# Loads issued from ScalarE's queue at written places, squares summed by DMA where rows are made, and a hand-written end, in a one-layer hybrid attention trunk

## The chip, the core and the metric

The kernel runs on one core of a Trainium2 chip. The core has TensorE (matrix products, fp32 in PSUM), VectorE, ScalarE, GpSimd and SyncE, called PE, DVE, ACT, POOL and SP in the profile, and 16 DMA engines. SP, ACT and POOL can issue transfers. The metric is the device time of one execution in microseconds (us); less is better.

## The reference, cut to what matters

The program is one layer of a decoder for 1024 positions and width 2048, in fp32:

```python
hn = rmsnorm(h, norm_mix_g)
sb_q, sb_k, sb_v, sb_g, df_q, df_k, df_v, df_g = split(hn @ w_in)
sb_out = stick_breaking_attention(sb_q, sb_k, sb_v)          # 8 heads of 128
df_out = rmsnorm(differential_attention(rope(df_q), rope(df_k), df_v, lam), subln_g)
mixed = concat([sb_out * silu(sb_g), df_out * silu(df_g)])
h = h + mixed @ w_out
gate = sigmoid(rmsnorm(h, norm_ple_g) @ w_ple_gate)
h = h + gate * (p @ w_ple_proj)
return rmsnorm(h, norm_final_g)
```

All the change touches, but for one line, lies behind the attention: the product with `w_out`, the gate with its norm, and the final norm. A norm needs the mean of the squares over all 2048 columns of a row of `h`.

## The kernel before, in words

Everything is kept transposed: a tile has 128 columns of the model on its partitions and 512 positions (a half) on its free axis. `h` is 16 such tiles ("rows" below) for each of two halves, in a DRAM tensor `h_d`. So a sum of squares over the width is a sum over 16 tiles and then over the partitions; the latter is a product with a matrix of ones (`norm`, `mean`).

**Products.** fp32 operands are split into a high part (a cast on ScalarE) and a low part (a subtraction on VectorE), and each product is three TensorE instructions: high by high, low by high, high by low. The large products (value and gate columns, `w_out`, `w_ple_gate`) use a scheme with seven block products in place of eight, named A11, A12, S2, S1, S3, A22 and S4; S1 to S4 are made of sums of operands or differences of weights (`T1` to `T4`). One block product of a unit is 4 by 3 = 12 instructions of 128x512.

**Stages.** (1) The value and gate columns (`gv`, to about 340 us). (2) Input projection and attention, to about 1790 us. (3) `w_out` (`op`, two passes `ph` of eight units `u`): pass 0 adds the first half of the width, pass 1 the second. In pass 1 each unit makes four finished rows of `h`, put to `h_d` by GpSimd's queue (`put`). `sums` makes the combinations S1 to S4 of these rows for the gate and stores them in `hcomb_d`. (4) The gate. Half 1's products A11 and A12 (`p1`, `p2`, `gate1`), then S2, S1, S4 (`p6`, `p5`, `p3`), then half 0's S3 and A22 (`begin` and the loop over six units). (5) The end: units 6 and 7 in quarters of 256 positions (`partly`), the final norm (`rstd_from`) and the outputs (`final`, `final1`).

**Order.** The class `Seven` holds the order. `prod` (or `gprod` in the gate) writes a product and then calls `step`: one more weight block is cast (`whigh`, ScalarE) and one block's low part made (`wlow`, VectorE), about six blocks ahead of use; then the entries of `soon` that are due run (`due`), and two or three entries of `xq`, the queue of operands to be split, each with the slot from which it may run. TensorE's order is as written all through (a `manual_schedule`), VectorE's and ScalarE's in stages 1, 3 and 4, too. SP's and GpSimd's order is made by a planner from modelled times and priorities, and in the end (from line 1955) so is VectorE's and ScalarE's. An engine runs its instructions in order, transfers it issues included: one that waits holds up all behind it.

**Places that the change and the steps touch.** Before the change:

- Line 1024 (`gv`) and line 1582 (`op`): in pass 0, the results `b` and `c` of a unit are two PSUM tiles of the pool `acc` if `u % 3 == 2`, otherwise the two halves of one tile `bc` (pool `z`). In unit 0 product S1 (into `c`) follows S2 (into `b`) directly; the sum `u2` (lines 1031, 1590) reads `b` after S2, and S3 goes on in `b`.
- `load_operand` (1281) issues an operand's load from SP. Lines 1621 to 1623 load the eight operands A11 and A12 of pass 1 in units 1 to 4.
- `gate_operand` and `gate_loads` (1303 to 1335) load the gate's operands from SP. For A11 and A12 their split also squares the row on ScalarE (1320, 1325) and adds it to `ssh[1]` on VectorE (the line 747 of the profile, from which `soon` is run). `NEXT` lists which loads follow which last product of pass 1.
- Lines 1627 to 1630 load four gate weight blocks (`second_load`) and the operands A12 4 to 7 and S1 0 to 3 behind the last product of pass 1.
- `squares0` (1729) loads a row of half 0 from `h_d` again, squares it on ScalarE, and `add_squares` (1669) adds it to `sq_d` by an accumulating transfer from GpSimd's queue.
- The end from line 1957: both quarters in a loop, with the eight outputs of the first quarter written by `final` between the second quarter's last products and its root.

Of the kernel before, what the change touches and what calls it, by code (L numbers as in the profile page):

```python
# [13 lines left out]
F32 = mybir.dt.float32  # L14
# [6 lines left out]
P = 128  # L21
# [31 lines left out]
def _body(ctx, nc, tc, ap):  # L53
# [491 lines left out]
    with tc.tile_pool(name="at", bufs=2) as at, tc.tile_pool(name="pz", bufs=2, space=PSUM) as pz:  # L545
# [461 lines left out]
        for ph in range(2):  # L1007
            for u in range(H):
# [269 lines left out]
        sq_d = dram.tile([2, 2, P, HALF], F32, name="sq_d", tag="sq_d")  # L1278
        SUMS = "S1", "S2", "S3", "S4"

        def load_operand(ph, nm, i):
# [6 lines left out]
            nc.sync.dma_start(lo.bitcast(F32), src)  # L1288
# [10 lines left out]
        NEXT = {"A11": [("A11", 0)], "A12": [("A12", 0)], "S1": [("A11", 4)], "S3": [("S2", 0)]}  # L1299
# [4 lines left out]
        def gate_operand(nm, i):  # L1304

            hi, lo = op.places(GPLACE[nm][i], "g" + nm)
            raw = lo.bitcast(F32)
# [6 lines left out]
            nc.sync.dma_start(raw, src)  # L1314

            def fn():
                if nm in ("A11", "A12"):
                    if 1 not in ssh:
                        ssh[1] = ev.tile([P, HALF], F32, name="ssh", tag="rstd1", bufs=1)
                        A.activation(ssh[1], raw, AF.Square)  # L1320
                    else:
                        for j in range(2):
                            o = slice(j * 2 * P, j * 2 * P + 2 * P)
                            s = ev.tile([P, 2 * P], F32, name="s", tag="sm", bufs=5)
                            A.activation(s, raw[:, o], AF.Square)
# [3 lines left out]
            return fn  # L1329

        def gate_loads(nm, i0):
            e = [(op.slot + 2, gate_operand(nm, i0 + j)) for j in range(4)]
# [4 lines left out]

        def put(o, ph, hf, ch):

            if ph:  # L1340
                G.dma_start(h_d[hf, ch], o)
            else:
# [223 lines left out]
        for ph in range(2):  # L1566
            for u in range(8):
# [14 lines left out]
                if ph == 0 and u % 3 == 2:  # L1582
# [83 lines left out]

        nsq = [0, 0]

        def add_squares(half, s):

            n = nsq[half]
            nsq[half] += 1
            G.dma_start(sq_d[half, n % 2], s, **(dict(accum_op=ALU.add) if n > 1 else {}))
# [55 lines left out]
        def squares0(n):  # L1729

            for ch in (n,):
                t = ev.tile([P, HALF], F32, name="hs", tag=("rstd0", "ssq")[n % 2], bufs=1)
                nc.sync.dma_start(t, h_d[0, ch])

                def fn(t=t):
                    A.activation(t, t, AF.Square)
                    add_squares(0, t)

                op.soon.append((op.slot + 3, fn))

# [4 lines left out]
        embedding_load(1, "f")  # L1745
        p1(2)
        gate_loads("S2", 4)
        p2(1)
        norm([ssh[1]])
# [7 lines left out]
        squares0(0)  # L1757
        p2(2)
        gate1(0)
        squares0(1)  # L1760
        p1(4)
        gate1(1)
        squares0(2)
        p2(3)
        gate1(2)
        squares0(3)
        p1(5)
        gate1(3)
        squares0(4)
        p2(4)  # L1770
        gate1(4)
        squares0(5)
        p1(6)
        squares0(6)
        p2(5)
        gate1(5)
        squares0(7)
        p1(7)
        second_places()
        squares0(8)  # L1780
        p2(6)
        gate1(6)
        squares0(9)
        p2(7)
        gate1(7)
        squares0(10)
# [34 lines left out]
        for u in range(8):  # L1821
# [3 lines left out]
            if 11 + u < 16:  # L1825
                squares0(11 + u)
# [42 lines left out]
        def final(ts, r):  # L1869
# [197 lines left out]
```

## Time and profile before

| what | value |
|---|---|
| median of 3 runs | 2481.51 us (2480.61 to 2482.8) |
| the profiled execution's own time | 2478.19 us |
| its span, first to last instruction | 2476.4 us |
| granted TensorE clock over the span | 0.988 |
| moved by DMA | 459.89 MB, mean 186 GB/s |

The span is the time from the first to the last instruction of the profiled execution; the rest of its own time lies around it. A line of the profile names a line of the kernel, an engine, an operation, what it writes and reads, and how often and how long. The granted clock is the share of TensorE's full clock that a throttle allowed; it falls to a half for a while after TensorE was idle.

### The profile page before, as it was taken

What the parts mean: (1) busy time and instruction counts of PE and PEld (TensorE: products, weight loads), DVE (VectorE), ACT (ScalarE), POOL (GpSimd) and SP (SyncE); (2) the same over time, 40 slices, a digit from 0 to 9 for tenths busy, and PEclk for the clock granted to TensorE, in tenths of its full rate; (3) what the DMA queues carried; (4) which work ended last, traced back from release to release, by engine and by line L of the source; (5) the groups of instructions that cost most, each with busy time, mean ns of one, the idle gap of its engine ahead of it and who ended that gap; (6) DMA issues with size and microseconds to landing.
All of it is one profiled execution on the core that took longest, in us unless ns stands there. A gap on an engine that the chain in (4) does not pass through costs nothing.

```text
span 2476.4 us, 32496 instructions
## 1 busy us (share of the span) xinstructions
PE 2374.1 (96%) x11250; PEld 1967.5 (79%) x11250; DVE 1905.4 (77%) x3288; ACT 1199.1 (48%) x2151; POOL 231.0 (9%) x353
## 2 busy tenths in 40 slices
PE   8999999999999999999999999998889998989997
PEld 5777878888888887888888888886768886868886
DVE  6788767777877778788888878778567888567787
ACT  5343335555556445555655555445423325532454
POOL 1211110000000000000000001110111110111100
PEclk9999999999999999999999999999989999999998
DMA  8776754443455556343443344555768768899964
GB/s 292 251 257 227 227 174 151 152 157 124 140 149 147 181 162 200 98 129 114 119 120 115 102 122 125 145 135 179 208 158 199 230 221 313 246 328 326 333 201 168
DMA packets 213828, 459.89 MB, mean 186 GB/s; under 512 B 23904, under 2 KB 36448, under 8 KB 213664
## 3 DMA queue, kind: packets, MB, share of 16 engines
q1 hardware_dynamic: 163696, 336.95, 41.6%
q0 software_dynamic: 41904, 106.19, 16.9%
q10 hardware_dynamic: 8064, 14.68, 1.6%
q8 instruction: 88, 1.44, 0.2%
q14 instruction: 76, 0.62, 0.1%
HBM read 323.51 MB, written 142.61 MB: 188 GB/s over the span
## 4 chain that ended last, share of the span: by engine, by line
PE 78%; DMA 8%; DVE 7%; ACT 3%; issue 3%; SPq 0%; POOL 0%; ACTq 0%; DVEq 0%; POOLq 0%
PE acc L227 13%; PE acc L229 13%; PE acc L228 13%; PE pbc L614 4%; PE pbc L616 4%; PE pbc L615 4%; PE tp L402 2%; PE z L306 1%; PE z L305 1%; PE pa L615 1%; PE pa L616 1%; PE pa L614 1%; PE av L449 1%; PE av L448 1%; PE pb L1639 1%
## 5 line engine op out<-in xcount | busy, mean ns | idle before, releaser
L227 PE MATMUL acc<-xh,whi 128*128 128x512 f32 x1152 | 465.2, 404 | 2.5 <-ACT xh L1104 2.5
L229 PE MATMUL acc<-xh,wlo 128*128 128x512 f32 x1152 | 451.3, 392 | 2.2 <-DVE wlo L154 2.2
L228 PE MATMUL acc<-xl,whi 128*128 128x512 f32 x1152 | 450.6, 391 | 0.3 <-DVE xl L1105 0.3
L154 DVE TENSOR_TENSOR wlo<-wraw,whi 128x1024 fp32r<-128x1024 f32 x192 | 234.2, 1220 | 48.5 <-ACT whi L153 47.1
L153 ACT CAST whi<-wraw 128x1024 fp32r<-128x1024 f32 x192 | 201.7, 1051 | 120.7 <-PE acc L228 112.0
L710 ACT CAST wpr<-T 128x512 fp32r<-128x512 f32 x144 | 87.3, 621 | 354.5 <-DVE T L669 289.5
L229 PEld LDWEIGHTS acc<-xh,wlo 128*128 128x128 f32 x1152 | 216.4, 188 | 51.1 <-DVE wlo L154 3.5
L227 PEld LDWEIGHTS acc<-xh,whi 128*128 128x128 f32 x1152 | 217.0, 188 | 40.6 <-ACT xh L1104 2.9
L228 PEld LDWEIGHTS acc<-xl,whi 128*128 128x128 f32 x1152 | 217.4, 189 | 37.9 <-DVE xl L1105 0.6
L421 ACT CAST awh<-tp 128x256 fp32r<-128x256 f32 (+1 forms) x160 | 80.7, 504 | 153.9 <-PE tp L402 153.9
L357 ACT ACTIVATE et<-z,mx 128x512 f32<-128x512 f32 (+7 forms) x128 | 94.7, 740 | 61.2 <-DVE mx L351 52.7
L710 ACT CAST wpr<-wraw 128x512 fp32r<-128x512 f32 x112 | 68.6, 614 | 105.6 <-DMA wraw<-tw_d 36.3
L426 DVE TENSOR_TENSOR awl<-tp,awh 128x256 fp32r<-128x256 f32 (+1 forms) x160 | 92.4, 578 | 32.2 <-ACT awh L421 31.9
L724 DVE TENSOR_TENSOR wpr<-T,wpr 128x512 fp32r<-128x512 f32 x144 | 98.7, 686 | 7.4 <-ACT wpr L710 6.1
L614 PE MATMUL pbc<-cS,wpr 128*128 128x512 f32 x224 | 88.4, 395 | 14.3 <-DVE u L1590 12.6
L351 DVE TENSOR_REDUCE mx<-z 128x1 f32<-128x512 f32 (+7 forms) x128 | 97.0, 758 | 4.4
L336 DVE TENSOR_TENSOR_SCAN st<-pt 128x511 f32<-128x511 f32 (+3 forms) x64 | 86.7, 1354 | 17.6 <-ACT pt L329 16.0
L724 DVE TENSOR_TENSOR wpr<-wraw,wpr 128x512 fp32r<-128x512 f32 x112 | 75.6, 685 | 21.9 <-ACT wpr L710 21.8
L615 PE MATMUL pbc<-cS,wpr 128*128 128x512 f32 x224 | 88.1, 393 | 0.0
L616 PE MATMUL pbc<-cS,wpr 128*128 128x512 f32 x224 | 88.1, 393 | 0.0
L449 PE MATMUL av<-awl,v 128*128 128x256 f32 x256 | 73.7, 288 | 9.0 <-DVE awl L426 9.0
L329 ACT ACTIVATE pt<-z 128x512 f32<-128x512 f32 (+3 forms) x64 | 41.6, 650 | 77.6 <-DVE z L313 72.1
(535 smaller groups left out, 6170.2 us busy)
## 6 DMA issues: line engine op xcount, KB each, us to landing
wraw<-w_in SPq DMA_DIRECT2D x192, 512.0 KB, 3.6
wraw<-w_gate SPq DMA_DIRECT2D x96, 256.0 KB, 6.0
wraw<-w_out SPq DMA_DIRECT2D x72, 256.0 KB, 4.0
wraw<-w_vg SPq DMA_DIRECT2D x71, 256.0 KB, 4.2
comb_d<-sg POOLq DMA_DIRECT2D x48, 256.0 KB, 7.2
h_d<-hc POOLq DMA_DIRECT2D x48, 256.0 KB, 4.5
spare<-xT SPq DMA_DIRECT2D x44, 256.0 KB, 3.9
hc<-h_d SPq DMA_DIRECT2D x33, 256.0 KB, 5.3
```

The lines of the kernel that those rows point to most:

```text
L153: side.later(1, lambda: A.copy(hi[:, o], raw[:, o]))
L154: side.later(side.wlo, lambda: V.tensor_tensor(lo[:, o], raw[:, o], hi[:, o].bitcast(F32), op=ALU.subtract))
L227: T.matmul(acc[c], hi[:, k2, kh, c, :], xh, start=first, stop=False)
L228: T.matmul(acc[c], hi[:, k2, kh, c, :], xl, start=False, stop=False)
L229: T.matmul(acc[c], lo[:, k2, kh, c, :], xh, start=False, stop=last)
L351: V.reduce_max(mx, z[:, vw], axis=AX.X, negate=True)
L449: T.matmul(av, vv[:, 0, blk % 4, :], wl, start=False, stop=last)
L614: T.matmul(o, wh[:, w], xh, start=start and k == 0, stop=False, skip_group_check=True)
L615: T.matmul(o, wh[:, w], xl, start=False, stop=False, skip_group_check=True)
L616: T.matmul(o, wl[:, w], xh, start=False, stop=k == 3, skip_group_check=True)
L710: A.copy(t[:, 0], src)
L724: V.tensor_tensor(t[:, 1], src, t[:, 0].bitcast(F32), op=ALU.subtract)
```

## The change

It has five parts.

1. In `gv` and `op`, pass 0 gives two separate PSUM tiles to units 0, 3 and 6 and not to 2 and 5.
2. Twenty-four loads are issued from ScalarE's queue, at the places where they stand in its written order: the eight operands of pass 1 (in units 1 to 4 of pass 0), the gate's operands S2 0 to 3, S2 4 to 7 and S1 0 to 3, and four gate weight blocks. The operands and the weight blocks stood before at the end of pass 1 (S2 4 to 7 after `p1(2)`), on SP's queue, and now stand after `p1(2)`, `plew(0, 0)`, `gate1(1)` and `gate1(3)`.
3. The squares of every row are made in pass 1, one slot after its `put` (`row_squares`), from the tile that is being stored, and added up in `sq_d` by accumulating transfers: half 1's in a new third place, half 0's in place 0. The squares and adds in `gate_operand` and all of `squares0` go. Half 1's sums are loaded as two tiles (`load_sums(2, ...)`) ahead of `norm`.
4. A11 and A12 of the gate are split three slots after their load, not two.
5. The end is in the manual order for VectorE and ScalarE, too: the four half-tiles of each quarter go step by step (`begun`, `sigm`, `ended`, `squared`), ScalarE's tables are loaded by name, four of half 1's outputs (`late`) and the first quarter's outputs are put between the steps, and unit 7's projection weights are loaded earlier.

```diff
-                if ph == 0 and u % 3 == 2:
+                if ph == 0 and u % 3 == 0:
-        sq_d = dram.tile([2, 2, P, HALF], F32, name="sq_d", tag="sq_d")
+        sq_d = dram.tile([3, 2, P, HALF], F32, name="sq_d", tag="sq_d")
-        def load_operand(ph, nm, i):
+        def load_operand(ph, nm, i, eng=nc.sync):
...
-            nc.sync.dma_start(lo.bitcast(F32), src)
+            eng.dma_start(lo.bitcast(F32), src)
...
-        NEXT = {"A11": [("A11", 0)], "A12": [("A12", 0)], "S1": [("A11", 4)], "S3": [("S2", 0)]}
+        NEXT = {"A11": [("A11", 0)], "A12": [("A12", 0)], "S1": [("A11", 4)]}
...
-            def fn():
-                if nm in ("A11", "A12"):
-                    if 1 not in ssh:
-                        ssh[1] = ev.tile([P, HALF], F32, name="ssh", tag="rstd1", bufs=1)
-                        A.activation(ssh[1], raw, AF.Square)
-                    else:
-                        for j in range(2):
-                            o = slice(j * 2 * P, j * 2 * P + 2 * P)
-                            s = ev.tile([P, 2 * P], F32, name="s", tag="sm", bufs=5)
-                            A.activation(s, raw[:, o], AF.Square)
-                            op.soon.append((op.slot + 1, partial(V.tensor_tensor, ssh[1][:, o], ssh[1][:, o], s, op=ALU.add)))
-                op.split("g" + nm, i, hi, lo, gain, apart=True)
+            eng.dma_start(lo.bitcast(F32), src)
+            return partial(op.split, "g" + nm, i, hi, lo, gain, apart=True)
-        def gate_loads(nm, i0):
-            e = [(op.slot + 2, gate_operand(nm, i0 + j)) for j in range(4)]
+        def gate_loads(nm, i0, eng=nc.sync):
+            e = [(op.slot + (3 if nm in ("A11", "A12") else 2), gate_operand(nm, i0 + j, eng)) for j in range(4)]
...
+        def add_squares(k, s):
+            n = nsq[k]
+            nsq[k] += 1
+            G.dma_start(sq_d[k, n % 2], s, **(dict(accum_op=ALU.add) if n > 1 else {}))
+
+        def row_squares(hf, o):
+            n = nsq[3]
+            nsq[3] += 1
+            t = ev.tile([P, HALF], F32, name="rsq", tag=f"rstd{n % 2}", bufs=1)
+            A.activation(t, o, AF.Square)
+            add_squares(2 * hf, t)
...
             if ph:
                 G.dma_start(h_d[hf, ch], o)
+                op.soon.append((op.slot + 1, partial(row_squares, hf, o)))
...
-                        xq.append((op.slot + 3, load_operand(1, nm, i)))
+                        xq.append((op.slot + 3, load_operand(1, nm, i, A)))
...
-            second_load(0, 0, b)
         gate_loads("A12", 4)
-        gate_loads("S1", 0)
...
+        sums2 = load_sums(2, ((ev, "rstd1", 1), (ev, "ssq", 1)))
         p1(2)
-        gate_loads("S2", 4)
+        gate_loads("S2", 0, A)
         p2(1)
-        norm([ssh[1]])
+        norm(sums2)
+        ssh[1] = sums2[0]
...
-        squares0(0)
+        gate_loads("S2", 4, A)
         p2(2)
         gate1(0)
         p1(4)
         gate1(1)
+        gate_loads("S1", 0, A)
         p2(3)
         gate1(2)
         p1(5)
         gate1(3)
+        for b in (12, 11, 22, 21):
+            A.dma_start(raws[0, 0, b], wg(0, 0, b))
...
+        partly(6, "A22", 1)
+        finals(0, (0,))
+        ended(6, 1, 1)
+        ended(7, 1, 1)
+        squared(6, 1, 1)
+        squared(7, 1, 1)
+        begun(6, 0, 1)
+        sigm(6, 0, 1)
+        partly(7, "A22", 1)
+        mean(1, (6, 1), (7, 1))
+        finals(0, (1, 2))
+        ended(6, 0, 1)
+        squared(6, 0, 1)
+        begun(7, 0, 1)
+        sigm(7, 0, 1)
+        tables(LOGS)
+        finals(0, (3,))
+        ended(7, 0, 1)
+        squared(7, 0, 1)
+        mean(1, (6, 0), (7, 0))
+        finals(0, (4, 5, 6, 7))
+        root(1)
+        finals(1, range(8))
```

In the end, `begun` adds the product to its other part and multiplies by the root of the gate's norm (two VectorE operations), `sigm` is the sigmoid (ScalarE), `ended` multiplies by the projected embedding and adds the row (two VectorE operations), and `squared` squares it (ScalarE, the last one VectorE).

More of the change, by code (lines that the diff above doesn't have):

```diff
@@ L1888, in fn @@
                 nc.sync.dma_start(ap["out"][ch * P:ch * P + P, HALF:], t)
-            op.soon.append((op.slot + 3, fn))
+            if u_ < 5:
+                op.soon.append((op.slot + 3, fn))
+            else:
+                late.append(fn)
+        late = deque()
         def gating0(u, c, o, z):
@@ L2013, in _body, with begun, sigm, ended @@
-        final(ts, r2)
+        def begun(u, c, tq):
+            ts = TQ[tq]
+            o = qs[u][c][:, ts]
+            V.tensor_tensor(o, b[u], o, op=ALU.add)
+            V.tensor_tensor(o, o, ssh[0][:, ts], op=ALU.mult)
+        def sigm(u, c, tq):
+            o = qs[u][c][:, TQ[tq]]
+            A.activation(o, o, AF.Sigmoid)
+        def ended(u, c, tq):
+            ts = TQ[tq]
+            o, t = qs[u][c][:, ts], hpair[u][:, c, ts]
+            V.tensor_tensor(o, o, z[u][:, c, ts], op=ALU.mult)
+            V.tensor_tensor(t, t, o, op=ALU.add)
@@ new lines, in squared, with mean @@
+        def squared(u, c, tq):
+            t = hpair[u][:, c, TQ[tq]]
+            s = sqs[u, c, tq] = ev.tile([P, Q], F32, name="sq", tag="sm", bufs=5)
+            if (u, c, tq) == (7, 0, 1):
+                V.tensor_tensor(s, t, t, op=ALU.mult)
+            else:
+                A.activation(s, t, AF.Square)
+        def mean(tq, *es):
+            first = tq not in ms
+            if first:
+                ms[tq] = pp.tile([P, Q], F32, name="ssps", tag="t")
+                T.matmul(ms[tq], ones, s2[:, TQ[tq]], start=True, stop=False)
+            for e in es:
+                T.matmul(ms[tq], ones, sqs.pop(e + (tq,)), start=False, stop=e == (7, 0))
@@ new lines, in tables, with root, finals @@
+        def tables(nm):
+            A.preload_act_table_set(nm)
+        r = ev.tile([P, HALF], F32, name="r2", tag="rstd1", bufs=1)
+        rt = ev.tile([P, HALF], F32, name="r3", tag="sq", bufs=2)
+        def root(tq):
+            rstd_from(ms[tq], 1.0 / NK, eps6, EPS, r[:, TQ[tq]], rt[:, TQ[tq]])
+        def finals(tq, us):
+            for u in us:
+                final(TQ[tq], r[:, TQ[tq]], u)
+        LOGS, SIGS = "natural_log_exp_and_others", "sigmoid_and_others"
+        partly(6, "S3", 0)
@@ new lines, in _body @@
+        for c in (1, 0):
+            ple(0, 6, c, z[6][:, c, :])
+        begun(6, 1, 0)
+        sigm(6, 1, 0)
+        partly(7, "S3", 0)
+        for c in (1, 0):
+            ple(0, 7, c, z[7][:, c, :])
+        begun(7, 1, 0)
+        ended(6, 1, 0)
+        late.popleft()()
+        squared(6, 1, 0)
+        sigm(7, 1, 0)
+        partly(6, "A22", 0)
+        ended(7, 1, 0)
+        late.popleft()()
+        begun(6, 0, 0)
+        squared(7, 1, 0)
+        sigm(6, 0, 0)
+        partly(7, "A22", 0)
@@ new lines, in _body @@
+        ended(6, 0, 0)
+        late.popleft()()
+        begun(7, 0, 0)
+        squared(6, 0, 0)
+        sigm(7, 0, 0)
+        tables(LOGS)
+        partly(6, "S3", 1)
+        ended(7, 0, 0)
+        squared(7, 0, 0)
+        late.popleft()()
+        begun(6, 1, 1)
+        partly(7, "S3", 1)
+        mean(0, (6, 1), (7, 1), (6, 0), (7, 0))
+        root(0)
+        tables(SIGS)
+        begun(7, 1, 1)
+        sigm(6, 1, 1)
+        sigm(7, 1, 1)
+        partly(6, "A22", 1)
+        finals(0, (0,))
```

123 lines of the change are left out of this document (31 added, 92 removed).

## The prediction, made before the result was known

> **What bounds the kernel now.** I read the page first, then the table of stretches (to see where TensorE falls short of its steady count), then TensorE's waits, and last the timelines around each wait.
>
> ```profile
> span 2476.4 us, 32496 instructions
> PE 2374.1 (96%) x11250; PEld 1967.5 (79%) x11250; DVE 1905.4 (77%) x3288; ACT 1199.1 (48%) x2151; POOL 231.0 (9%) x353
> ```
>
> TensorE is busy 96% of the span, and the diff removes none of its large products. So only the remaining holes can be won. Profile time is 2478.19 us (span 2476.4 and 1.8 around it). The median of the three runs is 2481.51, 3.3 us above; I make the sum against 2478.2 and add 3.3 at the end.
>
> ```profile
> 1780.00:1800.00 20.00, 12.97 (x59) 10.34 (x57) 6.67 (x11) 5.31 (x10) 4.30 (x5) 0.95 1.04 286
> 1800.00:1820.00 20.00, 13.71 (x50) 11.15 (x51) 12.94 (x21) 5.67 (x11) 0.84 (x1) 0.71 0.30 79
> ```
> ```profile
> 2060.00:2080.00 20.00, 15.53 (x60) 12.09 (x59) 15.98 (x31) 11.05 (x26) 2.32 (x5) 0.91 1.04 391
> 2080.00:2100.00 20.00, 15.22 (x57) 11.32 (x57) 17.23 (x33) 15.54 (x32) 0.00 (x1) 0.87 0.76 249
> ```
> ```profile
> 2120.00:2140.00 20.00, 20.00 (x90) 16.57 (x89) 12.94 (x23) 11.95 (x22) 3.08 (x5) 1.00 0.72 233
> ```
> ```profile
> 2180.00:2200.00 20.00, 16.00 (x64) 12.65 (x63) 10.53 (x18) 8.14 (x16) 3.07 (x4) 0.91 1.07 358
> 2200.00:2220.00 20.00, 14.77 (x56) 11.12 (x55) 18.34 (x31) 9.16 (x17) 4.59 (x7) 0.91 1.03 306
> ```
>
> Each row is a stretch of 20 us: busy time and count of PE, PEld, DVE, ACT and POOL, then granted clock, DMA share, GB/s. A full stretch holds 90 products (2120 to 2140), 0.222 us each. The stretch from 2060 holds 30 fewer (6.7 us lost), from 2080 33 fewer (7.3), from 2180 26 (5.8), from 2200 34 (7.6). In four of the six short stretches the DMA share is 1.03 or more: the holes sit where transfers queue.
>
> ```profile
> PE pbc L614 <- DVE u L1590: 12.6, 1, 12.6
> PE ssps L2004 <- ACT sq L2001: 5.5, 2, 4.4
> PE pa L1640 <- DVE cgA12l L601: 4.8, 3, 3.8
> PE pbc L614 <- DVE hq L1616: 4.7, 2, 3.7
> PE pb L1641 <- DVE wpr L724: 4.2, 2, 3.5
> PE z L1562 <- ACT pwhl L1554: 4.0, 1, 4.0
> ```
>
> These six names are nearly all of TensorE's waits after 1790 us. I call them hole A (u L1590), C (hq L1616), D (cgA12l), E (pwhl), F (wpr), and the tail (sq L2001).
>
> **The change, part by part.**
>
> *Two banks apart for unit 0 (`u % 3 == 0`).* In unit 0 the products S2 and S1 follow each other directly, and today their two results are halves of one tile. First the value-gate phase:
>
> ```profile
> 67.36 0.47 PE L614 MATMUL pbc<-cS,wpr 128*128 128x512 f32 x1 [1.33 <-ACT cS4h L593]
> ```
>
> This first product of S1 starts just after L1031 has read the other half; its own weights and operands were there before. The profile names an ACT cast that ended at the same moment, so I read the tile as the cause from the code. Apart, S1 goes at once and S3 behind it finds the read done: 1.3 us (between 0, if the cast was the cause, and 1.3).
>
> *Hole A: the same edit, and the eight loads that leave SP.*
>
> ```profile
> 1806.29 0.77 PE L614 MATMUL pbc<-cS,wpr 128*128 128x512 f32 x1 [12.64 <-DVE u L1590]
> ```
> ```profile
> 1811.54 0.39 PE L614 MATMUL pbc<-cS,wpr 128*128 128x512 f32 x1
> ```
>
> ```profile
> 1801.11 0.69 DVE L669 TENSOR_TENSOR T<-wraw 128x512 f32<-128x512 f32 x1 [8.51 <-issue]
> ```
> ```profile
> 1805.46 0.68 DVE L1590 TENSOR_TENSOR u<-pbc,s 128x512 f32<-128x512 f32 x1
> ```
>
> S1 waits for the sum L1590 in VectorE's order, and L1590 stands 5.0 us (1801.11 to 1806.14) behind a weight difference that waits for a `w_out` block. That block's transfer, among the issues of 1783 to 1792:
>
> ```profile
> cA11l<-mixed_d SPq DMA_DIRECT2D x4, 256.0 KB, 5.2
> cA12l<-mixed_d SPq DMA_DIRECT2D x4, 256.0 KB, 9.9
> ```
> ```profile
> wraw<-w_out SPq DMA_DIRECT2D x1, 256.0 KB, 10.6
> ```
>
> The block took 10.6 us behind eight operands of the second pass, which the planner had put ahead of it. After the change these eight are issued from units 1 to 4. What one load costs the 16 DMA engines comes from 2100 to 2200 us:
>
> ```profile
> q1 hardware_dynamic: 12421, 19.33, 57.9%
> q0 software_dynamic: 1904, 3.93, 19.7%
> ```
>
> 57.9 us for 19.33 MB is 0.785 us per 256 KB, so eight are 6.3 us. The difference starts at about 1795, L1590 ends at 1800.3, and S3, which truly needs that read, starts at 1800.5. Today S3 starts at 1811.54, after S1's twelve products at half speed. That is 11.0 us. S1 ends at 1796.3 (S2 ended at 1793.65, twelve products of 0.222 follow), and the 4.2 us left idle will still slow the clock: I take 1.8 us, which is what the clock of 0.91 costs in the 20 us from 2060, behind a hole of 3.7. That leaves 9.2. Bounds: 2.6 if the block lands as late as now (S1's 5.25 us fall into the hole, and S3's products are slow instead), 11.0 if none is slow.
>
> *Squares made where rows are made.* Holes C and D are where VectorE and ScalarE add up squares on arrival, today (2045 to 2100 us):
>
> ```profile
> L747 DVE TENSOR_TENSOR ssh<-ssh,s 128x256 f32<-128x256 f32 x30 | 11.3, 420 | 2.7 <-ACT s L1325 2.7
> ```
> ```profile
> L1325 ACT ACTIVATE s<-cgA12l 128x256 f32<-128x256 f32 x16 | 5.9, 406 | 4.3 <-DMA cgA12l<-h_d 2.8 <-DVE ssh L747 1.6
> ```
>
> All 30 adds go (11.3 us of VectorE), with their 30 half squares on ScalarE. Hole D is VectorE coming to the low parts of A12 late, by 3.8 us at the longest (the waits above). In the ten microseconds before them stand eight of these adds (11.3/30 each, 3.0 us) and the 1.6 us that ScalarE waited for their scratch. Both go, so I take 6.5 of 7.3; low end 2, because the sums S1 to S4 of units 6 and 7 still stand there and the split itself is put one product later (slot 3 for 2). In hole C the chain of three dependent operations remains:
>
> ```profile
> 2065.20 0.68 DVE L1612 TENSOR_TENSOR u<-pbc,s 128x512 f32<-128x512 f32 x1
> ```
> ```profile
> 2067.49 0.74 PE L614 MATMUL pbc<-cA,wpr 128*128 128x512 f32 x1 [3.68 <-DVE hq L1616]
> ```
>
> TensorE stopped at 2063.81 (2067.49 less 3.68), and the chain started 1.4 us later, behind a pair of such adds and two low parts. Without them the hole is about 2.4 us for 3.7. Whether the clock then still falls depends on where the hole lies; I count half of the 1.8 us. Together 2.2 (0 to 3.1).
>
> The Trainium skill ("TensorE: Matmul & The Clock Gate", Part 1) says TensorE's activity is judged in free-running windows of 3413 ns, at half clock after an idle one. One window at half speed would be 1.7 us (an estimate from that page), and the 1.8 us that the clock row from 2060 shows agree. By that rule hole C saves 3.1 or 1.3, by the luck of where the window lies, where the sum has 2.2.
>
> What it adds: 32 squares of 0.62 us on ScalarE in the mixing stage in place of as many later, and 16 more accumulating transfers, against 16 reads of 256 KB fewer. Row q0 above is the 16 accumulations of those 100 us:
>
> ```profile
> sq_d<-hs POOLq DMA_DIRECT2D x9, 256.0 KB, 5.9
> ```
> ```profile
> sq_d<-o POOLq DMA_DIRECT2D x7, 256.0 KB, 6.5
> ```
>
> They took 19.7 us of all 16 DMA engines, 1.23 us each. The 32 in the second pass of `w_out` are 39 us in some 165.
>
> ```profile
> 1920.00:2040.00 120.00, 118.98 (x525) 98.22 (x524) 100.91 (x157) 36.39 (x64) 13.89 (x25) 1.00 0.68 223
> ```
>
> There the DMA share is 0.68 and ScalarE is 30% busy; 0.68 + 0.24 is 0.92, so the cover holds, narrowly. One more tile in the mean of squares costs two matrix instructions, about 1.0 us:
>
> ```profile
> L1652 PE MATMUL ssps<-ssh,onesr 128*128 128x512 f32 x2 | 1.0, 592 | 0.0
> ```
>
> *Sixteen loads leave the turn from mixing to gate* (S2, S1 and four gate blocks). At 0.785 they are 12.6 us out of a stretch that is full, into 2100 to 2145, at share 0.72. I give them no price of their own: what they win is in D. *Holes E and F* lie in the gate stage at share 1.07:
>
> ```profile
> 2175.55 0.58 ACT L1713 COPY s<-paz 128x512 f32<-128x512 f32 x1 [4.96 <-DMA wraw<-w_gate]
> ```
> ```profile
> 2194.40 1.31 ACT L593 CAST cgS4h<-cgS4l 128x512 fp32r<-128x512 f32 x2 [6.45 <-DMA cgS4l<-hcomb_d]
> ```
>
> ScalarE, in order, waits for transfers, and the casts for TensorE come late. Removed there: each row's reload and its add (0.785 + 1.23 = 2.0 us), of which nine of 100 us, by the issues above, make some four in the 45 us up to 2200: 8 us. I let the transfers arrive 2 us earlier in each hole: E 2.2 of 5.8, F 3.3 of 7.6 (its clock too). Bounds 0 and 13.4 together: the eight blocks issued at once before E stay.
>
> *The end by hand.*
>
> ```profile
> 2455.41 0.28 PE L1967 MATMUL pbq<-cgA22h,wpr 128*128 128x256 f32 x1
> ```
>
> ```profile
> 2461.83 0.43 DVE L2003 TENSOR_TENSOR sq<-h 128x256 f32<-128x256 f32 x1
> ```
> ```profile
> 2466.96 3.70 DVE L1879 TENSOR_TENSOR h<-h,r 128x512 f32<-128x512 f32 x6
> ```
>
> From the last product (2455.7) to the last square (2462.3) pass 6.6 us, because all eight first-half outputs (3.70 for six of them, the last two through a line of their own) run in between. Four of them move behind the square, about half of that time. But VectorE still has two half-tiles to finish and three or four outputs in that stretch; adding its operations in the new order at up to 0.43 us each I get a last square 5.0 us after the last product, and one wait of TensorE less in the mean. Gain 2.5 (1 to 4). Behind it the root, eight outputs and the stores stay.
>
> **Sum:** 1.3 + 9.2 + 6.5 + 2.2 + 2.2 + 3.3 + 2.5 = 27.2 won; 1.0 for the mean; 3 for small new waits of ScalarE at 24 more issues (bounds 0 and the rival below). Net 23: 2478.2 − 23 = 2455.2 profiled, **2458.5** as a median. Its own range: all low ends (2.6 + 2 + 1, less 4, is 1.6) give 2479.9; all high ends (1.3 + 11.0 + 7.3 + 3.1 + 13.4 + 4, less 1, is 39.1) give 2442.4.
>
> **The rivals.** *The holes only move.* For it: the same bytes pass; E and F hang on the eight blocks that stay, and the moved loads fill 2100 to 2145. Against it: D's adds are gone for good. Then A gives 2.6, gate 1.3, D 2, tail 1, less 1 and 3: net 2.9, 2478.6.
>
> The Trainium skill ("DMA: Bandwidth & Descriptors", Issuing engines are not separate DMA queues) speaks for this rival: all queues run on the same 16 engines, so another issuer saves issue time only. The landings of 2100 to 2200 agree:
>
> ```profile
> hc<-h_d SPq DMA_DIRECT2D x9, 256.0 KB, 5.0
> ```
> ```profile
> h_d<-hc ACTq DMA_DIRECT2D x6, 256.0 KB, 4.6
> ```
>
> *ScalarE blocked by its own loads (slower).* Its queue is in order, and hole E shows what a transfer in front of casts does (row 2175.55: 4.96 us idle until a load that SP had issued). The change puts four groups of four loads into the gate stage and four pairs into `w_out`'s first pass, with weight casts, sigmoids and copies of the next units behind them. One such blockage costs what E costs, 5.8 us. Against it: casts run six products ahead, and tiles and sources are free at these places. It decides from four or five of the eight places: with five, 29.0 us lost against 26.2 won, 2484.3.
>
> *The accumulating transfers fill the second pass.* At 0.92 a share of 1.0 is near; two scratch tiles alternate, and the shortest distance between uses is three products of twelve (8.0 us), against 6.5 us of landing and 0.6 of square. If ScalarE waits 1.5 us in half of the 32 rows and half of that reaches TensorE, 12 us go (32 times 0.375): 2470.5.
>
> **How the numbers follow.** Forecast 0.55, holes move 0.20, ScalarE blocked 0.13, second pass full 0.12. About 0.2% (5 us) is what a measurement of this kernel tells from no change. Faster: 0.55 + 0.12 + 0.08 of the second = 0.75; same 0.12; slower 0.13. The range 2444 to 2481 leaves out the blocked case and the last of the best.
>
> **What would show it.** Hole A: S1 directly behind S2, the `w_out` block landing in some 5 us, a wait of about 4 before S3. D: no wait on cgA12l over 1 us. C about 2.4. E and F under 2.5 each. Second pass: DMA share near 0.92, 89 products per 20 us. Tail: under 19 us from the last product to the end (20.7 now). Wrong if new waits appear on ScalarE's casts between 2100 and 2150, or if VectorE reaches L1590 as late as now.

## The result, and the profile after

| kernel | median | lowest to highest | ratio to before, 95% interval |
|---|---|---|---|
| before (run beside it) | 2481.06 us, 4 runs | 2479.2 to 2482.8 | |
| after | 2462.94 us, 4 runs | 2462.04 to 2467.81 | 0.9931 [0.9914, 0.9948] |
| after, again, with another 11 runs of before | 2466.45 us, 6 runs | 2462.83 to 2471.49 | 0.9935 [0.9922, 0.9947] |

So the change wins 16 to 18 us. The profiled execution of after took 2463.29 us. Its page has nearly the same busy time on TensorE (2371.4 us for 2374.1) in a span 14.9 us shorter:

```profile
span 2461.5 us, 32426 instructions
PE 2371.4 (96%) x11252; PEld 1965.6 (80%) x11252; DVE 1896.0 (77%) x3257; ACT 1195.7 (49%) x2134; POOL 244.4 (10%) x369
```

The stretches of 20 us of after (columns as in the prediction: busy time and count of PE, PEld, DVE, ACT, POOL, then clock, DMA share, GB/s):

```profile
1780.00:1800.00 20.00, 15.05 (x68) 12.06 (x67) 8.04 (x14) 5.31 (x10) 4.30 (x5) 1.00 0.98 241
1800.00:1820.00 20.00, 16.31 (x63) 13.35 (x64) 14.34 (x24) 7.28 (x13) 1.71 (x2) 0.83 0.49 117
```
```profile
2060.00:2080.00 20.00, 17.15 (x71) 13.06 (x72) 13.20 (x20) 11.93 (x20) 4.26 (x6) 1.00 1.03 300
2080.00:2100.00 20.00, 17.45 (x76) 13.69 (x75) 11.40 (x18) 7.07 (x12) 0.00 (x0) 1.00 0.95 335
```
```profile
2160.00:2180.00 20.00, 16.14 (x64) 12.53 (x63) 11.43 (x19) 6.93 (x13) 0.84 (x1) 0.91 1.02 340
2180.00:2200.00 20.00, 17.33 (x74) 13.30 (x73) 16.99 (x29) 10.00 (x18) 2.84 (x4) 1.00 1.02 321
2200.00:2220.00 20.00, 20.00 (x90) 16.56 (x89) 15.91 (x27) 5.73 (x10) 2.56 (x4) 1.00 0.92 316
```

The two stretches around hole A now hold 131 products for 109, those of C and D 147 for 117. Those of E and F from 2180 on hold 164 for 120, but after is some 9 us ahead there, and its hole E lies in the stretch before. That one holds 64 for the 88 of before,

```profile
2160.00:2180.00 20.00, 19.85 (x88) 16.12 (x87) 9.90 (x16) 5.41 (x11) 2.03 (x4) 1.00 0.98 290
```

so all three together hold 228 for 208. TensorE's waits behind 1790 us, in after (us in total, times, longest):

```profile
PE pb L614 <- DVE u L1592: 7.5, 1, 7.5
PE pbc L614 <- DVE hq L1618: 3.9, 3, 2.3
PE z L1564 <- ACT pwhl L1556: 3.6, 1, 3.6
PE pa L1640 <- DVE cgA12l L601: 2.5, 2, 1.7
PE pb L1641 <- DVE wpr L724: 1.7, 2, 1.0
PE ssps L1985 <- DVE sq L1974: 1.5, 1, 1.5
```

All six names are still there: A 7.5 for 12.6, C with a longest wait of 2.3 for 3.7, E 3.6 for 4.0, D 2.5 for 4.8, F 1.7 for 4.2, and the tail with two waits of about 1.5 for 5.5 in all. Hole A did not close as forecast; this is its end in after:

```profile
1803.69 0.80 PE L614 MATMUL pb<-cS,wpr 128*128 128x512 f32 x1 [7.54 <-DVE u L1592]
```
```profile
1798.59 0.69 DVE L669 TENSOR_TENSOR T<-wraw 128x512 f32<-128x512 f32 x1 [6.22 <-DMA wraw<-w_out]
...
1802.95 0.68 DVE L1592 TENSOR_TENSOR u<-pb,s 128x512 f32<-128x512 f32 x1
```

S1 does follow S2 directly now (S3 is the first product with a wait), but VectorE's difference still waits for the `w_out` block. A view of the transfers issued at that moment, and of those issued in the 6 us before it, shows what may make the block late (queue, count, size, median us to landing):

```profile
wraw<-w_out SPq DMA_DIRECT2D x1, 256.0 KB, 8.7
```
```profile
comb_d<-sg POOLq DMA_DIRECT2D x3, 256.0 KB, 7.7
pw<-w_pp SPq DMA_DIRECT2D x5, 128.0 KB, 8.1
```

The eight operands are gone from there, but five loads of the embedding weights (`w_pp`, line 1550) have come in their place. In before the five scratch tiles that these loads go to (`sm`) were also used by the half squares of A11 and A12; with the squares made elsewhere the tiles are free as soon as attention ends, and the planner puts SP's loads for a stage 300 us later into this hole. I had not looked at that.

**Where each part went.** To place gains I compare the start of the n-th product of TensorE with that of the same product in before; a row is how much this difference changed over the stretch (positive is won). The two columns are two executions of the same kernel. Hole A is counted up to the end of the half-speed window behind it, the tail up to the end of the span.

| stretch | forecast | after | after, again |
|---|---|---|---|
| unit 0 of the value gate | 1.3 | 1.6 | 1.6 |
| from there to 1762 us, same code | 0 | -2.1 | -3.6 |
| hole A | 9.2 | 6.0 | 6.9 |
| `w_out` to its last unit | -3 | -1.1 | -3.7 |
| C, to the gate's first product | 2.2 | 1.8 | 1.3 |
| D | 6.5 | 4.8 | 4.9 |
| from D to 2140 us | -1 | -1.9 | -1.6 |
| E and F | 5.5 | 4.4 | 5.0 |
| from F to the last product | 0 | -0.5 | -0.7 |
| tail | 2.5 | 1.6 | 1.6 |

The columns add up to 14.6 and 11.7; the rest of the span's 14.9 and 12.2 lay ahead of the first row. (The forecast's 3 for new waits of ScalarE stands in the row of `w_out`, its 1.0 for the mean in the one behind D.)

### The profile page after: what moved, and what is told of

Same layout as the page of the kernel before. It is cut to its first block, busy times and chain, and to the rows that moved or that the text cites. A ratio compares the mean times of both kernels' runs of the same rounds, so it can differ in the third digit from the quotient of the medians.

```text
span 2461.5 us, 32426 instructions
## 1 busy us (share of the span) xinstructions
PE 2371.4 (96%) x11252; PEld 1965.6 (80%) x11252; DVE 1896.0 (77%) x3257; ACT 1195.7 (49%) x2134; POOL 244.4 (10%) x369
## 4 chain that ended last, share of the span: by engine, by line
PE 78%; DVE 8%; DMA 7%; issue 4%; ACT 3%; POOL 0%; SPq 0%; ACTq 0%; DVEq 0%; POOLq 0%
PE acc L227 13%; PE acc L229 13%; PE acc L228 13%; PE pbc L614 3%; PE pbc L616 3%; PE pbc L615 3%; PE tp L402 2%; PE z L306 1%; PE z L305 1%; PE pb L1639 1%; PE pb L1641 1%; PE pb L1640 1%; PE av L449 1%; PE pc L1639 1%; PE pc L1641 1%
## 5 line engine op out<-in xcount | busy, mean ns | idle before, releaser
L614 PE MATMUL pbc<-cS,wpr 128*128 128x512 f32 x208 | 81.0, 389 | 0.3 <-DVE u L1031 0.3
L616 PE MATMUL pbc<-cS,wpr 128*128 128x512 f32 x208 | 80.9, 389 | 0.0
L615 PE MATMUL pbc<-cS,wpr 128*128 128x512 f32 x208 | 80.9, 389 | 0.0
```

The source lines that it names most:

```text
L614: T.matmul(o, wh[:, w], xh, start=start and k == 0, stop=False, skip_group_check=True)
L615: T.matmul(o, wh[:, w], xl, start=False, stop=False, skip_group_check=True)
L616: T.matmul(o, wl[:, w], xh, start=False, stop=k == 3, skip_group_check=True)
```

## The experiments

Ratios are against runs of before beside them; 0.001 is 2.5 us.

| kernel | median | ratio, 95% interval |
|---|---|---|
| banks_alone | 2476.11 | 0.9974 [0.9964, 0.9984] |
| loads8_alone | 2477.06 | 0.9976 [0.9964, 0.9988] |
| squares_alone | 2485.53 | 1.0010 [1.0001, 1.0019] |
| gateloads_alone | 2488.52 | 1.0020 [1.0009, 1.0031] |
| squares_gateloads | 2478.28 | 0.9980 [0.9970, 0.9990] |
| end_alone | 2479.50 | 0.9987 [0.9978, 0.9997] |
| pw5_written | 2462.45 | 0.9911 [0.9896, 0.9926] |
| u2_first | 2464.89 | 0.9932 [0.9915, 0.9949] |
| pw5_order | 2461.71 | 0.9909 [0.9896, 0.9923] |
| stores_pool | 2459.06 | 0.9900 [0.9887, 0.9913] |
| pw5_order_stores | 2453.03 | 0.9880 [0.9867, 0.9894] |

### Hole A: the banks alone, the eight loads alone

```diff
-                if ph == 0 and u % 3 == 2:
+                if ph == 0 and u % 3 == 0:      # in gv and in op
```

> The kernel before with only the two tests u % 3 == 2 made u % 3 == 0, in the value-gate phase and in w_out. Theory (the banks and the loads need each other): the w_out block still lands in 10 to 11 us behind eight operands, so VectorE's weight difference still holds the sum L1590 and with it S3 until about 1811; S1's 12 products move ahead of the hole, S3's run at half speed, and hole A gives 2 to 3 us. The 1.3 us of the value-gate phase are back by 796 us, as in the kernel after. Time 2 to 3 us under the kernel before. Rival (the banks are the whole gain of hole A): S3 starts near 1804, 6 to 8 us under.

```diff
-                        xq.append((op.slot + 3, load_operand(1, nm, i)))
+                        xq.append((op.slot + 3, load_operand(1, nm, i, A)))
```

> The kernel before with only the eight operand loads of the second pass issued from ScalarE's queue in units 1 to 4 of the first. Theory (the banks and the loads need each other): the w_out block lands in about 8.6 us as in the kernel after, 2 us earlier than before, so L1590 ends 2 us earlier, and S1 and S3 follow it one after the other: 2 to 3 us under the kernel before. Rival (the loads are the whole gain of hole A): the block lands in about 5 us and the hole shrinks by 6 us. Rival (ScalarE is held by its own loads): new waits of TensorE on casts in the first pass, 0 to 3 us slower.

First products with a wait in hole A, and the landing of the `w_out` block, in banks_alone and then in loads8_alone:

```profile
1806.46 0.80 PE L614 MATMUL pb<-cS,wpr 128*128 128x512 f32 x1 [10.37 <-DVE u L1590]
```
```profile
wraw<-w_out SPq DMA_DIRECT2D x1, 256.0 KB, 11.1
```
```profile
1806.39 0.77 PE L614 MATMUL pbc<-cS,wpr 128*128 128x512 f32 x1 [6.98 <-DVE u L1590]
```
```profile
wraw<-w_out SPq DMA_DIRECT2D x1, 256.0 KB, 5.3
```

With the banks alone the block takes 11.1 us and hole A gives 2.5 us, as the theory and the prediction's lower bound of 2.6 had it (the whole kernel is 4 to 9 us under, of which more below). With the loads alone it lands in 5.3 us, as the prediction had said for the whole change, and hole A gives 6.8 us, as much as in after: the first rival was right, my expectation of 8.6 us was wrong. It had taken the landing in after for that of the loads' move, when the `w_pp` loads are in after only. No new wait of TensorE on a cast appears in the first pass, so ScalarE is not held there by its own loads. So the two do not need each other. Both together, with the block in time, should give about the sum, 9.3 us; pw5_written below is that case.

### The squares and the gate's loads, each alone and together

squares_alone takes `row_squares`, the third `sq_d` and `norm(sums2)` from after, drops `squares0` and the half squares in `gate_operand`, and splits A11 and A12 of the gate three slots after their load (part 4 of the change). gateloads_alone does this and no more (cut to what matters):

```diff
-        NEXT = {"A11": [("A11", 0)], "A12": [("A12", 0)], "S1": [("A11", 4)], "S3": [("S2", 0)]}
+        NEXT = {"A11": [("A11", 0)], "A12": [("A12", 0)], "S1": [("A11", 4)]}
...
-            second_load(0, 0, b)
...
-        gate_loads("S1", 0)
...
-        gate_loads("S2", 4)
+        gate_loads("S2", 0, A)          # each at its place in after
...
+        gate_loads("S2", 4, A)
...
+        gate_loads("S1", 0, A)
...
+        for b in (12, 11, 22, 21):
+            A.dma_start(raws[0, 0, b], wg(0, 0, b))
```

> The kernel before with only the squares made where rows are made (row_squares, sq_d of three, no squares0, no squares in gate_operand); all gate loads stay on SP at the old places. Theory (VectorE's adds are what hole D and part of C were): C and D give 5 us between 2045 and 2105, E and F 2 to 3 us more because sixteen reloads and their accumulations are gone from the gate stage, the second pass of w_out gives 1 to 1.5 us back to transfers at a share of 0.95. 6 to 8 us under the kernel before. Rival (hole D closes because sixteen loads leave the turn): D stays above 5 us, and the whole is 0 to 3 us under.

> The kernel before with only the gate loads moved: S2, S1 and four gate weight blocks issued from ScalarE's queue at written places behind the turn, the squares left as before. Theory (VectorE's adds are what hole D was): hole D keeps 5 us or more of its 7.3, E and F do not shrink, and the time is within 2 us of the kernel before. Rival (hole D closes because sixteen loads leave the turn): D under 3 us, 4 to 6 us under. Rival (ScalarE is held by its own loads): new waits of TensorE between 2100 and 2180, 2 to 6 us slower.

> The kernel before with the squares made where rows are made and the gate loads moved, both, but neither the banks nor the eight loads nor the end. Theory (each pays for the other: the squares alone fill the turn with reads and accumulations at once and lose 5 us at hole D, the moved loads alone lose 5 us at E and F behind the reloads of the squares): C and D together give 6 us, from 2100 on the gate stage gives 3 to 4 more, the second pass takes back 1 to 2, hole A stays at 13 us: 7 to 9 us under the kernel before, though each alone is slower. Rival (the two are additive): 2.5 and 5 us slower alone make 5 to 8 us slower together, or with their stage sums about nothing, and the 17 us of the whole change are the banks, the loads and the end.

Waits of TensorE in squares_alone, and what held ScalarE's split there:

```profile
PE pa L1642 <- ACT cgA L595: 7.3, 1, 7.3
```
```profile
2095.90 0.72 ACT L595 ACTIVATE cgA<-cgA,gvec 128x512 fp32r<-128x512 f32 x1 [8.40 <-DMA cgA<-h_d]
```

Waits in gateloads_alone at D, E and F:

```profile
PE z L1562 <- ACT pwhl L1554: 5.2, 1, 5.2
PE pb L1637 <- ACT wpr L710: 4.8, 1, 4.8
...
PE pa L1638 <- DVE cgA12l L601: 2.2, 2, 1.8
```

The turn from mixing to gate (2075 to 2110) in squares_alone, then gateloads_alone, and the gate stage (2150 to 2220) in the same two:

```profile
2075.00:2110.00 35.00, 24.41 (x87) 17.55 (x87) 17.68 (x28) 17.73 (x31) 4.20 (x6) 0.85 1.03 338
```
```profile
2075.00:2110.00 35.00, 32.02 (x135) 25.28 (x135) 24.61 (x46) 17.06 (x35) 1.08 (x2) 0.98 0.72 228
```
```profile
2150.00:2220.00 70.00, 67.49 (x290) 54.99 (x289) 44.24 (x73) 28.41 (x53) 6.83 (x9) 0.98 0.91 289
```
```profile
2150.00:2220.00 70.00, 54.06 (x219) 42.67 (x218) 37.06 (x61) 28.66 (x54) 12.49 (x15) 0.90 1.04 320
```

| stretch, us won against before | squares_alone | gateloads_alone | squares_gateloads |
|---|---|---|---|
| `w_out` to its last unit | -2.3 | 0.4 | -3.8 |
| C and D | -5.3 | 6.3 | 5.1 |
| from D to 2140 us | -0.8 | -2.3 | -2.6 |
| E and F | 9.4 | -8.3 | 4.4 |

This turns my step around. **Hole D** (4.8 us of waits in before) shrinks to 2.2 us in the kernel that keeps all thirty adds on VectorE, grows to 7.3 us on `cgA` and 3.4 on `cgA12l` in the one that has no adds, and is 3.6 us with both edits: it was the sixteen loads in the turn (share 1.03 against 0.72), not the adds. **Holes E and F** shrink when the reloads of the squares are gone (290 products from 2150 to 2220, at a share of 0.91, for 248 in before at 1.04) and grow when the moved loads come on top of them (219, at 1.04). So each edit alone pushes transfers into one place while clearing another, and is slower as a whole (by 0.1% and 0.2%, just clear of noise); together they are 5 us faster (2.5 to 7.5), where the two ratios alone add up to 7.5 us slower. The theory failed for both single kernels; for the pair it held in kind, not in size: the turn gave 5.1 us for 6, but from there to the end of F only 1.8 came (-2.6 and 4.4) for 3 to 4, and the second pass took 3.8 us for 1 to 2.

### The end alone

The edit is the end of the diff above, with `final`, `final1` and `plew_load(7)`.

> The kernel before with only the end written by hand. Theory (the hand-written order saves what the last square comes earlier): 4.9 us from the last product to the last square for 6.6, no new hole before it, 19.1 us from the last product to the end for 20.7: 1.6 us under the kernel before. Rival (it also frees the root): 18.2 us to the end, 2.5 us under. Rival (moving the loads of unit 7's weights and the last rows of half 1 costs more than it saves): holes before the last product, not under the kernel before.

The last square, in after:

```profile
2446.82 0.42 DVE L1974 TENSOR_TENSOR sq<-h 128x256 f32<-128x256 f32 x1
```

It ends 4.9 us behind the last product (2442.36) in after and in end_alone, 6.6 in before. VectorE's last outputs, in after:

```profile
2454.94 1.67 DVE L1847 SCALAR_TENSOR_TENSOR h<-h,gvec,r 128x256 f32<-128x256 f32 x4
```

They end 14.2 us behind the last product in all eight profiles with the new end, and 16.5 to 16.6 in all six with the old one; the store of the last output has landed after 17.4 to 17.5 us for 19.7 to 19.8. So the hand-written end gives 2.3 us in each of them. To the end of the span it looks like less, because what the span still holds behind that landing varies without the edit: 1.0 us in before and in end_alone, 1.7 in both executions of after, 1.3 to 1.8 in the others with the new end, 1.0 to 1.4 in the others with the old one. So it is 19.1 us from the last product to the end in after, 18.4 in end_alone and 20.7 in before, and end_alone's 2.3 us are near the rival's 2.5, not the expected 1.6. What makes this remainder stays open. The ratio of end_alone (0.7 to 5.5 us under) agrees and cannot tell 1.6 from 2.5.

### What is left of hole A

```diff
-                nc.sync.dma_start(pws[u, c], ap["w_pp"][u][:, :, c, :])
+                (A if len(pwn) < 5 else nc.sync).dma_start(pws[u, c], ap["w_pp"][u][:, :, c, :])
+                pwn.append(u)
```

> The kernel after, with the first five loads of the embedding weights (w_pp, 128 KB each) issued from ScalarE's queue at their written places in the gate stage, so that the planner can't issue them at 1783 to 1788 us, where the squares' scratch tiles have left their five tiles free. Theory (these five loads hold the w_out block): the block lands in 5 to 6 us for 8.65, the hole before S3 is 4 to 5 us for 7.5, and hole A gives 3 us more than in the kernel after. Rival (the accumulating transfers of that place hold it): the block still lands in over 8 us, no gain.

The landing and the hole in pw5_written:

```profile
wraw<-w_out SPq DMA_DIRECT2D x1, 256.0 KB, 5.0
```
```profile
1799.34 0.79 PE L614 MATMUL pb<-cS,wpr 128*128 128x512 f32 x1 [3.85 <-DVE u L1593]
```

Here hole A gives 9.2 us, the prediction's number, with its landing in 5 us and its wait of 4. The theory held here, but the five loads are not the whole of the late block. With them it took 8.7 us in after, 6.0 in its second execution, 5.8 in stores_pool and 5.3 in u2_first; without them 5.0 here and 5.3 and 4.3 in the two kernels with the same move below. The two groups touch at 5.3, and what makes the difference between executions stays open. The ratio against after (0.9911 and 0.9931 or 0.9935) is lower, with intervals that overlap.

The hole's other half is VectorE's order. u2_first makes one weight block fewer ahead (`op.lead(5)`), writes the sum `u2` before the weight difference, and puts unit 0's S4 before unit 1's S2:

```diff
-        op.lead()
+        op.lead(5)
...
+                if ph == 0 and u == 1:
+                    rest_of(prev, False)
-                prod(u, ph, "S2", b, True)
+                (product if ph == 0 and u == 0 else prod)(u, ph, "S2", b, True)
                 V.tensor_tensor(u2, b, s1, op=ALU.add)
+                if ph == 0 and u == 0:
+                    op.whigh()
+                    op.wlow()
+                    op.step()
...
-                    if prev:
+                    if prev and u > 1:
                         rest_of(prev, False)
```

> The kernel after with another written order in unit 0 of the first pass of w_out: one weight block fewer is made ahead, the sum u2 is written before the weight difference that waits for unit 1's block, and unit 0's S4 goes before unit 1's S2. Theory (VectorE's order makes the hole, the transfer only its length): S3 follows S1 at once, S4 follows, unit 1's S2 starts at about 1801.5 with its weights just made; the hole of 7.5 us and the 3.4 us of half speed go but for 1 or 2: 8 to 10 us under the kernel after. Rival (the late block only stops TensorE elsewhere): a hole of 3 us or more before unit 1's S2 or A22, with a slow window, 3 to 6 us under the kernel after.

```profile
1804.46 0.79 PE L614 MATMUL pb<-cS4h,wpr 128*128 128x512 f32 x1 [5.94 <-DVE hc L1624]
```

S3 no longer waits, but S4 does, 5.9 us: its result tile is still to be read by a sum (L1624) that is written behind the same weight work. The late block stops TensorE elsewhere, as the rival had it, and nothing is won over after (0.9932). pw5_order therefore leaves S4 where it was, writes `u3` and the row before the weight work as well (two `op.step()` behind them), and keeps the `w_pp` loads of pw5_written:

> The kernel pw5_written with another written order in unit 0 of the first pass of w_out: one weight block fewer is made ahead, the sums u2, u3 and the row that read unit 0's results are written before the weight work that waits for unit 1's block, S4 stays where it was. Theory (VectorE's order makes the hole, and in u2_first it only moved to S4, whose result tile was read late): no hole over 1 us between unit 0's S2 and unit 1's S2, at most 1.5 us before unit 0's A22, no slow window: 5 to 7 us under pw5_written. Rival (the late block stops TensorE anyway): a hole of 3 us before unit 1's S2, 0 to 2 us under pw5_written.

Waits of TensorE in pw5_order:

```profile
PE pbc L614 <- DVE hq L1624: 6.4, 6, 2.3
...
PE pbc L614 <- DVE u L1594: 1.1, 1, 1.1
```

Now the hole is gone but for 1.1 us, with no half-speed window there, and after unit 0 the kernel is 3.7 us further ahead than pw5_written. At the end it is not: 0.9909 and 0.9911. Up to the last unit of `w_out` it loses 3.8 us where pw5_written lost 1.2, and E takes the rest. In 120 us of the second pass, in after and in pw5_order:

```profile
1915.00:2035.00 120.00, 118.33 (x519) 96.54 (x518) 97.27 (x152) 46.55 (x84) 33.64 (x49) 1.00 0.94 265
```
```profile
1915.00:2035.00 120.00, 115.91 (x506) 94.33 (x506) 94.99 (x147) 44.28 (x80) 33.20 (x49) 1.00 0.93 257
```

At the same DMA share it makes 13 products fewer. The nine profiles with the squares in the second pass lose 1.1 to 4.0 us from hole A to the last unit of `w_out`, the other four gain 0.4 to 1.2. That what is won ahead of a stage with its transfers at 0.94 is lost in it fits this; that the transfers (and not ScalarE's added squares) are the reason was not tried apart.

### Holes E and F, and the best version

```diff
-                A.dma_start(tw_d[u, 0][:, ks, :], b12)
+                G.dma_start(tw_d[u, 0][:, ks, :], b12)
```

and the same for the other half of `tw_d`, for `part_d` and for the finished rows of half 1.

> The kernel after, with ScalarE's stores of the gate stage (the weight differences tw_d, the partial products part_d, the finished rows of half 1) issued from GpSimd's queue. Theory (hole E is ScalarE standing still behind its own stores, each of which waits until a transfer that SP issued before it has landed): ScalarE's casts of the operands and of the embedding weights come 2 to 4 us earlier, the hole before the embedding product is under 1 us for 3.6, and 3 to 5 us go. Rival (the casts wait for their own loads at a DMA share of 1.02): E stays above 2.5 us, no gain.

> The two kernels before it together: w_pp loads at their written places, the order of unit 0, and ScalarE's stores of the gate stage from GpSimd's queue. Theory: what each gives adds up, since they lie 350 us apart: 8 to 12 us under the kernel pw5_written, near 2450 us. Rival (GpSimd's transfers cost more of the engines than ScalarE's and the gate stage is full): no better than pw5_order.

One copy of a finished product on ScalarE, in after with the two stores ahead of it, and in stores_pool:

```profile
2164.51 0.33 ACTq L1456 DMA_DIRECT2D tw_d<-wraw  x1
2165.84 0.33 ACTq L1457 DMA_DIRECT2D tw_d<-wraw  x1
2166.21 0.58 ACT L1705 COPY s<-paz 128x512 f32<-128x512 f32 x1 [3.91 <-DMA wraw<-w_gate]
```
```profile
2156.24 0.59 ACT L1705 COPY s<-paz 128x512 f32<-128x512 f32 x1 [0.61 <-PE paz L1641]
```

The copy needs nothing from `w_gate`. It stood behind two stores of ScalarE's queue. In the trace each of them waits for a semaphore on which a `w_gate` load that SP had issued counts its landing: the first load landed at 2164.48 and the first store went out at 2164.51, the second at 2165.82 and 2165.84. With the stores on GpSimd's queue the copy waits 0.6 us, for its product. Hole E is 1.2 us in stores_pool (under 1 was named), and the kernel is 0.9900: 8 us under after, more than the 3 to 5 expected. Of these the profile places some 5 in E and F (9.6 us won there for 4.4 and 5.0 in after). The gate stage from 2140 to 2200, in pw5_order and in pw5_order_stores:

```profile
2140.00:2200.00 60.00, 52.82 (x220) 41.87 (x219) 42.72 (x71) 24.95 (x47) 6.81 (x9) 0.97 1.00 314
```
```profile
2140.00:2200.00 60.00, 56.51 (x242) 45.95 (x241) 44.20 (x73) 24.44 (x46) 15.86 (x26) 0.97 1.00 333
```

Both kernels come to 2140 at the same product within 0.2 us, and at a share of 1.00 in both the second makes 22 more: it was not the transfers' capacity but who waited for them. Theory right in kind, rival wrong, though E itself stays at 2.5 us in pw5_order_stores. **pw5_order_stores** is 8 us under pw5_written by the ratios and 9 by the medians, at the low end of the 8 to 12 expected, with the stores' part paying more than said and the order's nothing. It beats before by 30 us and after by 10 to 13.

### The kernel after once more

> The kernel after, unchanged, once more. Theory (the clock's half-speed windows fall by chance): gaps of TensorE within 1 us of the first profile of it in the places A, C, D, E, F and the tail, but the half-speed windows before 1790 us at other places, and spans that differ by several us for that alone. Rival (the windows belong to the kernel): the windows near 193 and 354 us are there again.

The same three stretches of 3.4 us in after, then in its second execution:

```profile
190.03:193.44 3.41, 1.49 (x7) 0.95 (x6) 3.15 (x7) 2.03 (x5) 0.54 (x1) 1.00 0.96 312
193.44:196.86 3.42, 3.42 (x9) 2.65 (x8) 3.35 (x6) 0.40 (x1) 0.00 (x0) 0.50 0.46 173
351.76:355.18 3.42, 2.58 (x9) 2.08 (x10) 1.92 (x2) 0.00 (x0) 0.00 (x0) 0.81 0.64 170
```
```profile
190.03:193.44 3.41, 1.53 (x7) 0.98 (x6) 3.41 (x7) 2.03 (x4) 0.54 (x1) 1.00 0.92 300
193.44:196.86 3.42, 2.72 (x13) 1.88 (x12) 3.35 (x6) 0.00 (x0) 0.54 (x1) 1.00 0.46 165
351.76:355.18 3.42, 3.42 (x10) 2.64 (x9) 0.68 (x1) 0.00 (x0) 0.00 (x0) 0.50 0.82 244
```

TensorE waits at the same places both times; which wait is followed by a half-speed window differs. The window at 193 us was not there again, that near 354 was at 352. The rival fails. The places agree and their waits within 2 us (1 was expected), but for hole A (7.5 and 4.9).

## Why the prediction was right or wrong

Forecast 2458.5, measured 2462.9 and 2466.5: the sign, the order of size and the range held; 16 to 18 us came for 23. Some parts came near their number for another reason than the one given.

- **Two banks in the value gate, 1.3:** right, 1.6. The wait is gone, and with it the first product's 0.47 us for 0.39.
- **Hole A, 9.2:** the mechanism was right, but after gave 6.0 and 6.9. pw5_written shows the number to the tenth, with some luck: its S3 came 11.6 us earlier for the 11.0 named, and the half-speed window behind the hole took 2.4 for 1.8 (2.1 and 3.0 in after). The step that failed is "the block lands in some 5 us": I let the eight loads leave and did not ask what the planner would put there, though another part of the change frees five tiles. It landed in 8.7 and 6.0 us, and that these five loads are the whole reason is not shown.
- **D, 6.5:** 4.8, and for another reason. "Both go, so I take 6.5 of 7.3" put the hole down to the adds on VectorE; the runs put it down to the sixteen loads, which I had priced at nothing of their own. That the sum is near is luck: the loads left in the same change. "No wait over 1 us" failed (1.7).
- **C, 2.2:** 1.3 to 1.8; the wait is 2.3 us for the 2.4 named.
- **E and F, 5.5:** 4.4 and 5.0, and the reason held: reloads and accumulations gone. "Under 2.5 each" failed for E in the first execution (3.6) and for F in the second (2.9, a single wait). "The eight blocks issued at once before E stay" was half of what stays; the other half, ScalarE's own stores, stood in the quoted row of the copy's 4.96 us, and I took that for a wait on the load itself.
- **Tail, 2.5:** right in mechanism and nearly in size: the last square is 4.9 us behind the last product (5.0 named), and the last output lands 2.3 us sooner. The span shows 1.6 of it and 19.1 us where "under 19" was named, because 0.7 us more lie behind that landing, which the prediction took as fixed.
- **New waits and the mean, 4:** 3.5 and 6.0 (the three negative rows behind A). They are not ScalarE's at its own loads. In the second pass the DMA share is 0.94 for the 0.92 forecast, with 519 products in 120 us (86.5 per 20 us for 89). The accumulating transfers were priced too low: over 1920 to 2040 us GpSimd's queue took 17.7% of the 16 engines in before and 47.7% in after, with 25 of them there, which makes about 1.5 us each (an estimate from these shares) for 1.23. The rival "second pass full" had the place and direction; its 12 us were at least three times too many.
- **The rivals:** "holes only move" would have left D; gateloads_alone shows its mechanism at work (D won, E and F lost) and squares_alone its mirror, and only the two together escape it. "ScalarE blocked by its own loads" did not show; ScalarE was blocked by its stores.
- **3.3 us added at the end** was too little. The 72 runs of before in these comparisons lie between 2478.2 and 2490.1 us: the profiled one (2478.19) is faster than all of them. Between 60 and 1790 us it had only two half-speed windows; the other thirteen profiles have two to six.

One gap stays open. Against the profile of before, the 1.6 us of the value gate are gone by 796 us in after and in banks_alone (0.1 and 0.0 left). But up to 1762 us, where only the banks of the value gate differ, the five other kernels without that edit are 1.9 to 6.7 us behind before, and the eight with it lie between 1.5 us ahead and 1.4 behind. The 1.6 us of unit 0 explain less than half of that; the rest may be the chance of the windows or the planner's order, and no run tells which. banks_alone fits the larger gain (6.5 us, 4 to 9, of which hole A is 2.5).

## What to carry to other kernels

When a part of a change frees buffers, ask which planned transfer can now start earlier, and where it will land: it went straight into the hole that another part was meant to clear. Put a hole down to an engine's work only when the same stretch with fewer transfers has been looked at; here the adds beside the hole were innocent, and two edits that each lose alone won together because each had been paying for the other's transfers. A store on the queue of an engine that casts for the critical path can make that engine wait: moving ScalarE's stores gave 8 us here, moving the eight loads 6 (3 to 9).

## What the runs showed of the hardware that I had not expected

The clock's windows have a fixed grid of 3.413 us that lies differently in each execution. In before, half-speed windows start at 1712.53, 1726.18 and 2067.52 us, which are 4 and 100 such steps apart; in after one starts at 193.44, in its second execution one at 351.76 (rows above), which is 46.4 steps later. A window needs no full idleness to slow the next: in the rows above, 1.49 us of TensorE in 3.41 (44%) were followed by one at 0.50. Over the fourteen profiles (some 9,400 full-speed windows between 60 and 2400 us, counted from the traces) every one in which TensorE was busy for less than 44% was followed by a half-speed window, none with more than 50% was, and between them both occur. The Trainium skill ("TensorE: Matmul & The Clock Gate", Part 1) has the length and the free running, which agree, and an idle window as the cause, where these rows show a half-idle one. So a wait of 1.9 us costs nothing or another 1.7 us by where it falls.

Plain stores issued by GpSimd were no dearer for the kernel than ScalarE's: with them the gate stage moved 333 GB/s for 314 (the two rows at 2140 to 2200).
